# A two-layer diffusion block on one core: the start of the program rearranged (S5 loads, projection weights, modulation)

## The chip, the cores and the metric

The kernel runs on one core of one Trainium2 chip, as one program. The metric is the device time of one execution in microseconds (us). Before the change three runs took 2019.58, 2006.54 and 2016.45 us, median 2016.45. The engines are TensorE (PE), VectorE (DVE), ScalarE (ACT), GpSimd (POOL) and SyncE (SP). SP issues most transfers. ACT has a transfer queue of its own, and both queues issue in the order of their engine's instruction list.

## The reference

One latent stream of 512 tokens and a context of 256 tokens, 1024 wide, pass two layers. Layer 0 mixes with RWKV-7 heads and S5 channel groups that share one input projection `w_in`, layer 1 with latent attention; each layer ends in a mixture of experts. What matters here is the start of layer 0:

```
m_l = split(silu(c)     @ mod_w[0] + mod_b[0], 6)   # shift, scale, gate, ... for latent tokens
m_c = split(silu(c_ctx) @ mod_w[0] + mod_b[0], 6)   # the same for context tokens
a   = rmsnorm(h) * (1 + scale) + shift
p   = a @ w_in                                      # (768 x 1024) @ (1024 x 1792+512)
lam_bar = exp(lam * dt);  b_bar = ((lam_bar - 1) / lam) * b     # S5, per group of 16 channels
```

Everything is float32. `lam`, `dt`, `b` and `c` of S5 are small tables (2 directions, 32 groups, 64 states, 16 channels): 256 KB for each part of `b` and of `c`.

## The kernel before

The kernel is written in a tile framework that plans the order: the order in which the source calls operations sets priorities, and a planner with simulated times decides in which order the instructions then stand on each engine. Within one engine (and one queue) that order is fixed and is kept on the chip, whatever is ready.

`front` (L1795) runs the start. The 768 tokens are six tiles of 128 rows. For each tile: SP loads x (L1811, four buffers), ACT squares and sums it (L207), DVE and ACT make the reciprocal root (L217 to 221), ACT scales the rows (L1815), PE turns the tile in eight 128x128 transposes into two PSUM banks (L271, name nx), and ACT copies one half to `xT` (L276), DVE the other (L274).

Between tiles 2 and 3 `mod_part(0, 0)` (L139) stands: 16 loads of 512 KB of `mod_w` (name mw, L161, three buffers), each followed by four matmuls into one PSUM bank (psmod, L163); then DVE adds the bias and multiplies by the norm's weight (mo, L166 and L168), SP stores the result to DRAM (mods, L170), and `modcols` (L262) loads it back with channels on partitions (mcol).

`s5_tables` (L782) loads the S5 parameters through ACT's queue (L788 to L891), computes on DVE a long chain of small operations on 128x32 tiles (edt, emag, pw, co), then on 128x512 the product of `co` with `b` (s5tm, s5bb, L775 to L780), and turns the parts of c on PE (s5tc, L869). Before, `b` is loaded as 128 x 32 x 16, in pieces of 64 bytes.

`norm_mod` (L278) applies scale and shift to `xT` on POOL, 16 operations, and then splits each of eight channel blocks into a rounded high part (aT, ACT, L183) and a low part (DVE, L184). With aT the projection `w_in` starts: four blocks of weights (wi, L315, 512 KB each, two buffers), split in the same way (wih on ACT, wil on DVE), three matmuls per product into pwi (L189 to L191), and DVE's convolution into q (L327, L329).

After that come the S5 quads and 14 projection blocks, `mod_part(0, 1)` and `(0, 2)`, the RWKV stages (until about 940 us), `mod_part(1, 0..2)` inside the last of them (48 more loads of mw in the window 760 to 915 us), the output projection, the experts and layer 1.

Of the kernel before, what the change touches and what calls it, by code (L numbers as in the profile page):

```python
# [3 lines left out]


# [2 lines left out]

# [8 lines left out]
F32 = mybir.dt.float32  # L17
# [69 lines left out]
class Block:  # L87
# [50 lines left out]
    def mod_part(self, l, q, wpool, spool, tag="mod"):  # L138

        nc, i = self.nc, self.i  # L140
        if l not in self.mods:
            self.mods[l] = self.dr.tile([2, 6 * D], F32, name=f"mods{l}")
        dst = self.mods[l]
        mb = spool.tile([128, 512], F32, name=f"mb{l}{q}", tag="mb", bufs=1)
        nc.gpsimd.memset(mb, 0.0)
        for v in range(2):
            nc.sync.dma_start(mb[v::32, :], dap(i["mod_b"], l * 6 * D + q * 2048, [[512, 4], [1, 512]]))
        if q != 1:
            gm = spool.tile([128, 512], F32, name=f"gm{l}{q}", tag="gm", bufs=1)
            nc.gpsimd.memset(gm, 1.0)  # L150
            r0 = 64 if q == 0 else 0
            for v in range(2):
                nc.sync.dma_start(gm[r0 + v:r0 + 64:32, :], dap(i["norm1_g" if q == 0 else "norm2_g"], l * D,
                                                                [[512, 2], [1, 512]]))
            nc.vector.tensor_scalar(mb[r0:r0 + 64, :], mb[r0:r0 + 64, :], 1.0, None, op0=OP.add)
        ps = self.psum(tag, f"psmod{l}{q}", 1)
        for k in range(8):
            for h in range(2):
                wt = wpool.tile([128, 4, 256], F32, name=f"mw{l}{q}{k}{h}", tag="mw")
                w = i["mod_w"][l, k * 128:(k + 1) * 128, q * 2048:q * 2048 + 2048].rearrange("p (j c) -> p j c", j=4)  # L160
                nc.sync.dma_start(wt, w[:, :, 256 * h:256 * h + 256])  # L161
                for j in range(4):
                    nc.tensor.matmul(ps[32 * j:32 * j + 32, 256 * h:256 * h + 256], self.cst[:, k, :], wt[:, j],  # L163
                                     start=(k == 0 and h == 0), stop=(k == 7), skip_group_check=True)
        mo = spool.tile([128, 512], F32, name=f"mo{l}{q}", tag="mo", bufs=1)
        nc.vector.tensor_tensor(mo, ps, mb, OP.add)  # L166
        if q != 1:
            nc.vector.tensor_tensor(mo, mo, gm, OP.mult)  # L168
        for v in range(2):
            nc.sync.dma_start(dap(dst, v * 6 * D + q * 2048, [[512, 4], [1, 512]]), mo[v::32, :])  # L170

    def bcast(self, pool, l, v, c, name, tag, bufs):
        t = pool.tile([128, D], F32, name=name, tag=tag, bufs=bufs)
# [84 lines left out]
    def modcols(self, l, pool):  # L258

        t = pool.tile([128, 2, 2, 8], F32, name=f"mcol{l}")  # L260
        for v in range(2):
            self.nc.sync.dma_start(t[:, v], dap(self.mods[l], v * 6 * D, [[8, 128], [D, 2], [1, 8]]))  # L262
        return t

    def norm_x(self, xT, xn, t):

        nc = self.nc
        for h in range(2):
# [4 lines left out]
            if h:  # L273
                nc.vector.tensor_copy(dst, src)  # L274
            else:
                nc.scalar.activation(dst, src, AF.Copy)  # L276

    def norm_mod(self, aT, xT, mc):  # L278

        nc = self.nc  # L280
        for k in range(8):
            for v, c in ((1, slice(0, CTX)), (0, slice(CTX, T))):
                nc.gpsimd.tensor_scalar(xT[:, k, c], xT[:, k, c], mc[:, v, 1, k:k + 1], mc[:, v, 0, k:k + 1],
                                        op0=OP.mult, op1=OP.add)
            self.split(aT[0][:, k], aT[1][:, k], xT[:, k])

    def norm_tile(self, x, r, t, mc, pool):
# [18 lines left out]
                self.split(aT[0][:, ks], aT[1][:, ks], p3)  # L306
        return aT

    def w_in(self, aT, ms, wpool, hpool, qpool, done):

        nc, i = self.nc, self.i
        w = i["hy_w_in"]
        for m in ms:
            wt = wpool.tile([128, 8, 128], F32, name=f"wi{m}", tag="w")
            nc.sync.dma_start(wt, w[0, :, m * 128:(m + 1) * 128].rearrange("(p k) c -> p k c", k=8))  # L315
            wh = hpool.tile([128, 8, 128], F32R, name=f"wih{m}", tag="wh")
            wl = hpool.tile([128, 8, 128], F32R, name=f"wil{m}", tag="wl")
            self.split(wh, wl, wt)
# [463 lines left out]
    def s5_tables(self, cp, tp):  # L782
# [57 lines left out]
        self.a8 = self.c0.tile([128, 32], F32, name="s5a8")  # L840
        nc.vector.tensor_copy(self.a8, mag[:, 32:64])

        b = [tp.tile([128, 32, 16], F32, name=f"s5b{k}") for k in range(2)]
        for k, nme in enumerate(("s5_b_re", "s5_b_im")):
            nc.scalar.dma_start(b[k], dap(i[nme], 0, [[16, 128], [2048, 32], [1, 16]]))
        co = [tp.tile([128, 32], F32, name=f"s5co{k}") for k in range(2)]
        den = tp.tile([128, 32], F32, name="s5den")
        nc.vector.tensor_tensor(den, lr, lr, OP.mult)
# [946 lines left out]
    def front(self, qd, es):  # L1795
# [5 lines left out]
        with ExitStack() as e0:  # L1801
# [3 lines left out]
            with ExitStack() as e1:  # L1805
# [1 line left out]
                self.cond(xp)  # L1807
                xT = xp.tile([128, 8, T], F32, name="xT")
                for t in range(6):
                    xt = xp.tile([128, D], F32, name=f"x{t}", tag="x", bufs=4)  # L1810
                    nc.sync.dma_start(xt, self.src_rows(t))  # L1811
                    if t == 3:
                        self.mod_part(0, 0, mp, ms)
                    r = self.rstd_of(xp, xt, f"n0{t}")
                    nc.scalar.activation(xt, xt, AF.Copy, scale=r)  # L1815
                    self.norm_x(xT, xt, t)
                self.prep_cols(xp)
                self.s5_tables(c5, self.pool("s5p", 1, es=e1, side="right"))
                self.norm_mod(aT, xT, self.modcols(0, xp))
            wp = self.pool("wpb", 2, es=e0)  # L1820
            w5 = self.pool("s5w", 1, es=e0, side="right")
# [3 lines left out]
            rt = self.pool("s5rt", 1, es=e0, side="right")  # L1825
            self.s5_quad(0, w5)
            self.s5_quad(1, w5)
            self.w_in(aT, MS14[4 * 0:4 * 0 + 4], wp, hp, qp, take)
            self.s5_rot(rt)
            self.w_in(aT, MS14[4 * 1:4 * 1 + 4], wp, hp, qp, take)  # L1830
            self.mod_part(0, 1, mp, ms)
# [288 lines left out]
```

## Time and profile before

| what | value |
|---|---|
| runs | 2019.58, 2006.54, 2016.45 us (median 2016.45) |
| profiled execution | 2017.53 us, span 2015.5 us |
| TensorE's mean granted clock | 0.855 of full speed |
| busy share of the span | PE 79%, DVE 62%, POOL 39%, ACT 38% |
| transfers | 350.79 MB, mean 174 GB/s |
| `mod_w` loads | 96 of 512 KB, the largest group of transfers |

The shares are means over stages with different limits, so each stage is read by itself: in the first 100 us no engine is busy throughout, from 100 to 200 us DVE is, from 250 to 300 us PE is. A timeline row gives start, duration, engine (a q behind the name is that engine's transfer queue), line, operation, output and inputs, count, and in brackets the idle time before it and what ended it.

### The profile page before, as it was taken

The numbers are of one execution on the slowest core, as the hardware profiler recorded it, in microseconds if no ns is written. First come the engines' busy times: TensorE is split into PE (matmuls) and PEld (weight loads), VectorE is DVE, ScalarE is ACT, GpSimd is POOL, SyncE is SP. The second block draws the span as 40 slices with busy tenths as digits, with TensorE's granted clock in tenths as the row PEclk, the third lists the DMA queues.
The fourth block names the chain that finished last, engine by engine and source line by source line (L and its number), as shares of the span: only waits on it lengthen the run. The fifth ranks groups of instructions, "written<-read, shape, count | busy, mean of one in ns | idle before, by whom it ended". The sixth has DMA issues, their size and how long they took to land. (4 is left out here: it accounts for less than half of the span.)

```text
span 2015.5 us, 32393 instructions
## 1 busy us (share of the span) xinstructions
PE 1588.1 (79%) x12499; PEld 1151.5 (57%) x12499; DVE 1247.4 (62%) x2353; ACT 768.4 (38%) x1374; POOL 778.5 (39%) x732
## 2 busy tenths in 40 slices
PE   3688898477865857764979899967789998788993
PEld 2376767366755744433856666636655555666662
DVE  3799733986669485426365555657677874565554
ACT  4222323343443432213131554632456543325552
POOL 0577802572546351110333323534124444414432
PEclk9688899558967976876979999987879998889997
DMA  8654677723323316776631799963000006539974
GB/s 228 191 175 139 212 244 212 216 71 91 93 66 86 91 48 195 236 243 205 229 142 60 284 382 347 369 227 134 1 0 1 0 1 259 201 115 356 375 261 178
DMA packets 232581, 350.79 MB, mean 174 GB/s; under 512 B 57794, under 2 KB 178552, under 8 KB 217576
## 3 DMA queue, kind: packets, MB, share of 16 engines
q1 hardware_dynamic: 208944, 297.89, 44.3%
q0 software_dynamic: 10080, 44.04, 6.1%
q10 hardware_dynamic: 13400, 6.75, 1.2%
q8 instruction: 100, 1.64, 0.3%
q14 instruction: 57, 0.47, 0.1%
HBM read 280.60 MB, written 68.03 MB: 173 GB/s over the span
## 5 line engine op out<-in xcount | busy, mean ns | idle before, releaser
L163 PE MATMUL psmod<-mw,cst 128*32 128x256 f32 x768 | 81.6, 499 | 46.8 <-DMA mw<-in_mod_w_dram 46.7
L189 PE MATMUL pwi<-aT,wih 128*128 128x512 f32 (+1 forms) x224 | 83.4, 374 | 12.0 <-DVE q L329 12.0
L571 POOL TENSOR_TENSOR G<-G,gmask 128x1024 f32<-128x1024 f32 x24 | 58.9, 2458 | 80.7 <-ACT G L570 80.5
L191 PE MATMUL pwi<-aT,wil 128*128 128x256 f32 (+1 forms) x224 | 81.8, 366 | 0.0
L190 PE MATMUL pwi<-aT,wih 128*128 128x256 f32 (+1 forms) x224 | 81.6, 365 | 0.0
L1079 PE MATMUL s5y<-s5tq,s5H 128*96 128x128 f32 x256 | 52.4, 351 | 31.4 <-POOL s5H L1071 17.8
L1751 ACT ACTIVATE P<-st 128x512 f32<-128x512 f32 x96 | 56.9, 596 | 49.5 <-PE st L1749 46.1
L1382 POOL DMA_INDIRECT xg<-fbuf,rk x36 | 37.6, 1043 | 96.4 <-PE ptx L229 57.3
L1764 POOL TENSOR_TENSOR sum<-sum,P 128x512 f32<-128x512 f32 x48 | 63.6, 1348 | 28.2 <-ACT P L1751 28.0
L163 PEld LDWEIGHTS psmod<-mw,cst 128*32 128x32 f32 x768 | 19.9, 124 | 89.7 <-DMA mw<-in_mod_w_dram 65.9
L183 ACT ACTIVATE xT<-ptx 128x512 fp32r<-128x512 f32 x72 | 41.2, 596 | 68.1 <-PE ptx L229 67.7
L567 PE MATMUL pg<-PQ,KB 64*128 64x128 f32 x384 | 51.2, 352 | 14.9 <-ACT ta L496 10.1
L1079 PEld LDWEIGHTS s5y<-s5tq,s5H 128*96 128x96 f32 x256 | 41.4, 216 | 37.5 <-POOL s5H L1071 20.5
L184 DVE TENSOR_TENSOR xT<-ptx,xT 128x512 fp32r<-128x512 f32 x72 | 48.1, 687 | 22.1 <-ACT xT L183 21.2
L1762 POOL TENSOR_TENSOR sum<-P,P 128x512 f32<-128x512 f32 x16 | 20.5, 1301 | 106.5 <-ACT P L1751 106.4
L189 PEld LDWEIGHTS pwi<-aT,wih 128*128 128x128 f32 x224 | 47.1, 212 | 22.8 <-issue 13.7
L728 POOL TENSOR_TENSOR vo<-vo,bsum 128x512 f32<-128x512 f32 x6 | 6.2, 1042 | 134.3 <-DMA vo<-vtok 125.9
L229 PEld LDWEIGHTS ptx<-ident,xg 128*128 128x128 f32 x288 | 41.1, 193 | 28.0 <-issue 22.1
L567 PEld LDWEIGHTS pg<-PQ,KB 64*128 64x128 f32 x384 | 43.9, 244 | 22.2 <-ACT ta L496 10.4
L1755 PE MATMUL po<-P,vv 128*64 128x512 f32 x192 | 54.3, 617 | 1.1 <-ACT P L1751 1.1
L229 PE MATMUL ptx<-ident,xg 128*128 128x128 f32 x288 | 43.4, 286 | 12.4 <-issue 8.3
L190 PEld LDWEIGHTS pwi<-aT,wih 128*128 128x128 f32 x224 | 46.9, 209 | 6.8 <-issue 1.6
(1564 smaller groups left out, 5254.0 us busy)
## 6 DMA issues: line engine op xcount, KB each, us to landing
mw<-in_mod_w_dram SPq DMA_DIRECT2D x96, 512.0 KB
yb<-yo SPq DMA_DIRECT2D x36, 512.0 KB
s5tq<-s5t SPq DMA_DIRECT2D x16, 960.0 KB
yb<-zrow SPq DMA_DIRECT2D x16, 512.0 KB
wi<-in_hy_w_in_dram SPq DMA_DIRECT2D x14, 512.0 KB
rk<-qbuf SPq DMA_DIRECT2D x12, 512.0 KB
fbuf<-f SPq DMA_DIRECT2D x10, 512.0 KB
s5t<-s5CP SPq DMA_DIRECT2D x4, 1152.0 KB
```

The source lines that it names most:

```text
L163: nc.tensor.matmul(ps[32 * j:32 * j + 32, 256 * h:256 * h + 256], self.cst[:, k, :], wt[:, j], start=(k == 0 and h == 0), stop=(k == 7), s ...
L184: nc.vector.tensor_tensor(lo, src, hi.bitcast(F32), OP.subtract)
L189: nc.tensor.matmul(out, lh, rh, start=start, stop=False, **kw)
L190: nc.tensor.matmul(out, lh, rl, start=False, stop=False, **kw)
L191: nc.tensor.matmul(out, ll, rh, start=False, stop=stop, **kw)
L229: nc.tensor.transpose(pt[:, k * 128:(k + 1) * 128], a[:, h * 4 + k::8], self.ident)
L567: nc.tensor.matmul(pg[hp][:, m], KB[rs, m, ps2], PQ[rs, m, ps2], start=True, stop=True, skip_group_check=True)
L571: nc.gpsimd.tensor_tensor(G[:, par], G[:, par], self.mask[:, z, par, None, :].to_broadcast([128, 8, 128]), OP.mult)
L1079: nc.tensor.matmul(out, H[:, g, d, k, h0:h0 + 96], CP[:, k, d, i0:i0 + 8, :].rearrange("p a b -> p (a b)"), start=False, stop=(d == 1 and ...
L1751: ex = nc.scalar.activation(P, st, AF.Exp, scale=SCALE)
L1755: mm = nc.tensor.matmul(po[64 * x:64 * x + 64], vv[:, kt, h0 + x, :], P, start=(kt == 0), stop=(kt == 5), skip_group_check=True)
L1764: nc.gpsimd.tensor_tensor(sums[x], sums[x], P, OP.add)
```

## The change

- The transfers of `s5_tables` are all placed behind the last ACT copy of the input norm (`issue_after(normed)`), on ACT's queue as before.
- `b` is loaded as 32 rows of 8 KB and turned by 2 x 16 transposes on PE into two PSUM banks of tag "tp", from which DVE then reads it.
- The first four projection weights are issued behind the last load of `mod_part(0, 0)`.
- The six x tiles have six buffers in place of four.
- The store of mods and the load of mcol of this first part go through ACT's queue in place of SP's.
- `norm_mod` works on DVE for even channel blocks and on POOL for odd ones.

```diff
@@ mod_part
-                nc.sync.dma_start(wt, w[:, :, 256 * h:256 * h + 256])
+                last = nc.sync.dma_start(wt, w[:, :, 256 * h:256 * h + 256])
...
-            nc.sync.dma_start(dap(dst, v * 6 * D + q * 2048, [[512, 4], [1, 512]]), mo[v::32, :])
+            (nc.sync if l + q else nc.scalar).dma_start(dap(dst, v * 6 * D + q * 2048, [[512, 4], [1, 512]]), mo[v::32, :])
+        return last.ins
@@ modcols
-            self.nc.sync.dma_start(t[:, v], dap(self.mods[l], v * 6 * D, [[8, 128], [D, 2], [1, 8]]))
+            (self.nc.sync if l else self.nc.scalar).dma_start(t[:, v], dap(self.mods[l], v * 6 * D, [[8, 128], [D, 2], [1, 8]]))
@@ norm_mod
         for k in range(8):
+            eng = nc.gpsimd if k % 2 else nc.vector
             for v, c in ((1, slice(0, CTX)), (0, slice(CTX, T))):
-                nc.gpsimd.tensor_scalar(xT[:, k, c], xT[:, k, c], mc[:, v, 1, k:k + 1], mc[:, v, 0, k:k + 1],
-                                        op0=OP.mult, op1=OP.add)
+                eng.tensor_scalar(xT[:, k, c], xT[:, k, c], mc[:, v, 1, k:k + 1], mc[:, v, 0, k:k + 1],
+                                  op0=OP.mult, op1=OP.add)
@@ w_in
-            nc.sync.dma_start(wt, w[0, :, m * 128:(m + 1) * 128].rearrange("(p k) c -> p k c", k=8))
+            with self.tc.issue_after(behind) if behind is not None else nullcontext():
+                nc.sync.dma_start(wt, w[0, :, m * 128:(m + 1) * 128].rearrange("(p k) c -> p k c", k=8))
@@ s5_tables
-        b = [tp.tile([128, 32, 16], F32, name=f"s5b{k}") for k in range(2)]
+        b = []
         for k, nme in enumerate(("s5_b_re", "s5_b_im")):
-            nc.scalar.dma_start(b[k], dap(i[nme], 0, [[16, 128], [2048, 32], [1, 16]]))
+            raw = tp.tile([32, 2048], F32, name=f"s5br{k}")
+            nc.scalar.dma_start(raw, dap(i[nme], 0, [[2048, 32], [1, 2048]]))
+            pt = self.psum("tp", f"s5tb{k}", 2)
+            for c in range(16):
+                nc.tensor.transpose(pt[:, c * 32:c * 32 + 32], raw[:, c::16], self.ident[:32, :32])
+            b.append(pt.rearrange("p (c n) -> p n c", n=32))
@@ front
-                    xt = xp.tile([128, D], F32, name=f"x{t}", tag="x", bufs=4)
+                    xt = xp.tile([128, D], F32, name=f"x{t}", tag="x", bufs=6)
...
-                        self.mod_part(0, 0, mp, ms)
+                        loads = self.mod_part(0, 0, mp, ms)
...
-                    self.norm_x(xT, xt, t)
+                    normed = self.norm_x(xT, xt, t)
...
-                self.s5_tables(c5, self.pool("s5p", 1, es=e1, side="right"))
+                with self.tc.issue_after(normed):
+                    self.s5_tables(c5, self.pool("s5p", 1, es=e1, side="right"))
...
-            self.w_in(aT, MS14[4 * 0:4 * 0 + 4], wp, hp, qp, take)
+            self.w_in(aT, MS14[4 * 0:4 * 0 + 4], wp, hp, qp, take, loads)
```

The planner rearranges much behind these few lines: the lists of all engines differ from the start to about 940 us, and are alike from there on. Three places carry the prediction.

First ACT in the norm. Before (s5b and s5cr are transfers of b and c, x ... n00r the scaling of a tile, xT the copy of a turned tile):

```order
L207 ACTIVATE n02q,n02s<-x_161 128x1024
L845 DMA s5b_508<-in_s_b_re_dram 128x32x16
L845 DMA s5b_509<-in_s_b_im_dram 128x32x16
L868 DMA s5cr_541<-in_s_c_re_dram 128x1x64
L276 ACTIVATE xT<-nx_123 128x4x128
L1815 ACTIVATE x_135<-x_135,n01r 128x1024
```

Now, the end of the norm on ACT and what follows:

```order
L277 ACTIVATE xT<-nx_339 128x4x128
L1824 ACTIVATE x_351<-x_351,n05r 128x1024
L277 ACTIVATE xT<-nx_365 128x4x128
L792 DMA s5rows<-in_s_lam_re_dram 32x128
L793 DMA s5rows<-in_s_lam_im_dram 32x128
L795 DMA s5ld<-in_s_log_dt_dram 32x2
L850 DMA s5br_508<-in_s_b_re_dram 32x2048
L850 DMA s5br_527<-in_s_b_im_dram 32x2048
L877 DMA s5cr_575<-in_s_c_re_dram 128x1x64 x2
```

The transfers of S5 stood between the first and the second copy of the norm, and stand now behind the sixth. Further down on ACT come one split (wih), the store of mods, a second split, the load of mcol, the eight splits of aT, and then eight transfers of the imaginary part of c.

Second DVE around the modulation. Before:

```order
L775 TENSOR_TENSOR s5tm_486<-s5b_508,s5co_512 128x512
L776 TENSOR_TENSOR s5tm_487<-s5b_509,s5co_513 128x512
L166 TENSOR_TENSOR mo_296<-psmod_199,mb_190 128x512
L777 TENSOR_TENSOR s5bb_530<-s5tm_486,s5tm_487 128x512
L168 TENSOR_TENSOR mo_296<-mo_296,gm_194 128x512
L778 TENSOR_TENSOR s5tm_486<-s5b_508,s5co_513 128x512
L779 TENSOR_TENSOR s5tm_487<-s5b_509,s5co_512 128x512
L780 TENSOR_TENSOR s5bb_531<-s5tm_486,s5tm_487 128x512
```

Then came four small ones for the heads and the eight low parts of aT. Now:

```order
L779 TENSOR_TENSOR s5tm_486<-s5tb_510,s5co_546 128x512
L780 TENSOR_TENSOR s5tm_487<-s5tb_529,s5co_547 128x512
L286 TENSOR_SCALAR xT<-xT,mcol_633 128x512 x4
L781 TENSOR_TENSOR s5bb_564<-s5tm_486,s5tm_487 128x512
L286 TENSOR_SCALAR xT<-xT,mcol_633 128x256 x4
L782 TENSOR_TENSOR s5tm_486<-s5tb_510,s5co_547 128x512
L783 TENSOR_TENSOR s5tm_487<-s5tb_529,s5co_546 128x512
L185 TENSOR_TENSOR aT_83<-xT,aT_82 128x768 x3
L784 TENSOR_TENSOR s5bb_565<-s5tm_486,s5tm_487 128x512
L185 TENSOR_TENSOR aT_83<-xT,aT_82 128x768 x5
L889 COPY s5dg<-s5td 128x8
```

DVE's half of the modulation stands inside the work on b. The two operations of mo, and two splits wil of projection weights, now stand earlier, inside the chain of small operations; behind aT stand s5dg and the small ones for the heads, the first product with c (s5q) and the first convolution (q).

Third SP at the end of the RWKV stages. Before:

```order
L161 DMA mw_9142<-in_mod_w_dram 128x4x256
L701 DMA yd_2712<-Y_8902 64x512
L701 DMA yd_2713<-Y_8902 64x512
L161 DMA mw_9148<-in_mod_w_dram 128x4x256
L161 DMA mw_9154<-in_mod_w_dram 128x4x256
L161 DMA mw_9160<-in_mod_w_dram 128x4x256
L734 DMA yo_9006<-yd_2713 128x512
L1902 DMA cz_9215<-s5buf 128x768
L161 DMA mw_9166<-in_mod_w_dram 128x4x256
```

Now:

```order
L161 DMA mw_9194<-in_mod_w_dram 128x4x256
L161 DMA mw_9200<-in_mod_w_dram 128x4x256
L705 DMA yd_2746<-Y_8837 64x512
L705 DMA yd_2747<-Y_8837 64x512
L170 DMA mods_7875<-mo_9206 4x512 x2
L705 DMA yd_2746<-Y_8936 64x512
L705 DMA yd_2747<-Y_8936 64x512
L738 DMA yo_9040<-yd_2747 128x512
```

yd and yo are the outputs of the last RWKV steps. The last 10 of the 48 loads of mw stood behind the store of the last step but one; now all 48 stand ahead of it. On PE the last eight groups of psmod stood behind all matmuls of RWKV and now stand ahead of the last step's.

## Rows read from the trace of the kernel before

**Rows 1.** timeline of ACT and its queue: start, us, operation, idle before

```profile
10.77 5.21 ACTq L845 DMA_DIRECT2D s5b<-in_s_b_im_dram  x1
...
16.02 8.44 ACTq L868 DMA_DIRECT2D s5cr<-in_s_c_re_dram  x1
24.51 0.60 ACT L276 ACTIVATE xT<-nx 128x512 f32<-128x512 f32 x1 [12.70 <-issue]
...
33.57 0.60 ACT L276 ACTIVATE xT<-nx 128x512 f32<-128x512 f32 x1 [0.22 <-PE nx L271]
...
42.59 0.60 ACT L276 ACTIVATE xT<-nx 128x512 f32<-128x512 f32 x1 [0.80 <-PE nx L271]
...
46.25 5.61 ACTq L868 DMA_DIRECT2D s5cr<-in_s_c_im_dram  x7
```

**Rows 2.** timeline of SP's queue

```profile
37.24 2.56 SPq L315 DMA_DIRECT2D wi<-in_hy_w_in_dram  x2
39.91 25.02 SPq L161 DMA_DIRECT2D mw<-in_mod_w_dram  x13
...
66.50 1.08 SPq L170 DMA_DIRECT2D mods<-mo  x2
...
69.97 0.89 SPq L262 DMA_DIRECT2D mcol<-mods  x2
```

**Rows 3.** timeline of PE

```profile
44.58 0.53 PE L795 MATMUL s5t<-ident,s5rows 32*128 32x32 f32 x3
...
46.19 1.08 PE L163 MATMUL psmod<-mw,cst 128*32 128x256 f32 x8
...
63.42 1.08 PE L163 MATMUL psmod<-mw,cst 128*32 128x256 f32 x8 [0.34 <-DMA mw<-in_mod_w_dram]
...
69.77 1.08 PE L163 MATMUL psmod<-mw,cst 128*32 128x256 f32 x8 [0.75 <-DMA mw<-in_mod_w_dram]
```

**Rows 4.** timeline of DVE

```profile
10.94 0.42 DVE L155 TENSOR_SCALAR mb<-mb 64x512 f32<-64x512 f32 x1 [1.11 <-DMA mb<-in_mod_b_dram]
...
40.46 0.89 DVE L894 TENSOR_TENSOR s5glu<-s5gw,s5m 128x128 f32<-128x128 f32 x4
...
45.14 0.26 DVE L797 COPY s5lam<-s5t 128x96 f32<-128x96 f32 x1 [0.23 <-PE s5t L795]
...
62.34 0.29 DVE L780 TENSOR_TENSOR s5pw<-s5tm,s5tm 128x128 f32<-128x128 f32 x1
...
64.56 0.69 DVE L166 TENSOR_TENSOR mo<-psmod,mb 128x512 f32<-128x512 f32 x1 [0.60 <-PE psmod L163]
...
80.66 8.99 DVE L184 TENSOR_TENSOR aT<-xT,aT 128x768 fp32r<-128x768 f32 x8 [11.54 <-ACT aT L183]
...
97.39 0.47 DVE L327 SCALAR_TENSOR_TENSOR q<-pwi,cols,q 128x255 f32<-128x255 f32 x1
```

**Rows 5.** groups of DVE by shape, 30 to 100 us: count, busy, mean ns, idle

```profile
L184 DVE TENSOR_TENSOR wil<-wi,wih 128x1024 fp32r<-128x1024 f32 x2 | 2.5, 1225 | 1.0 <-ACT wih L183 1.0
```

**Rows 6.** timeline of POOL

```profile
73.21 14.58 POOL L283 TENSOR_SCALAR xT<-xT,mcol 128x512 f32<-128x512 f32 x16 [6.17 <-DMA mcol<-mods]
```

**Rows 7.** groups of POOL by shape, 60 to 100 us

```profile
L283 POOL TENSOR_SCALAR xT<-xT,mcol 128x256 f32<-128x256 f32 x8 | 8.6, 1085 | 0.0
L283 POOL TENSOR_SCALAR xT<-xT,mcol 128x512 f32<-128x512 f32 x8 | 6.0, 764 | 6.2 <-DMA mcol<-mods 6.2
```

**Rows 8.** windows: length, busy of PE, PEld, DVE, ACT, POOL, clock, DMA share, GB/s

```profile
100.00:125.00 25.00, 20.75 (x128) 16.58 (x128) 25.00 (x44) 7.30 (x12) 20.84 (x18) 1.00 0.56 191
...
250.00:300.00 50.00, 50.00 (x320) 34.34 (x319) 15.03 (x27) 11.79 (x23) 4.81 (x8) 1.00 0.77 231
...
850.00:900.00 50.00, 37.12 (x652) 21.56 (x652) 19.61 (x42) 10.22 (x20) 5.07 (x5) 0.76 0.76 237
```

**Rows 9.** timeline of SP's queue at the end of RWKV

```profile
901.62 5.28 SPq L161 DMA_DIRECT2D mw<-in_mod_w_dram  x3
```

**Rows 10.** waits of PE, 760 to 940 us: total us, times, longest

```profile
PE psmod L163 <- DMA mw<-in_mod_w_dram: 30.7, 20, 5.0
```

More of the change, by code (lines that the diff above doesn't have):

```diff
@@ L6 @@
 import math
-from contextlib import ExitStack
+from contextlib import ExitStack, nullcontext
 import concourse.bacc as _bacc
@@ L275, in norm_x @@
             else:
-                nc.scalar.activation(dst, src, AF.Copy)
+                last = nc.scalar.activation(dst, src, AF.Copy)
+        return last.ins
     def norm_mod(self, aT, xT, mc):
@@ L307, in norm_tile, with w_in @@
         return aT
-    def w_in(self, aT, ms, wpool, hpool, qpool, done):
+    def w_in(self, aT, ms, wpool, hpool, qpool, done, behind=None):
         nc, i = self.nc, self.i
```

## The prediction

> **What bounds the kernel now.** I read the windows first, because the busy shares of the page mix stages. From 100 to 125 us DVE is busy all 25.00 us, and from 250 to 300 us PE is busy all 50.00 us [rows 8]. So whatever makes the first 100 us shorter is passed on: DVE starts its full stretch earlier, and PE its own after it. Then I read the timelines of the first 100 us, engine by engine, looking for the operation that lets DVE begin on aT, and going back from there.
>
> The low parts of aT start on DVE at 80.66 and end at 80.66 + 8.99 = 89.65, after an idle time of 11.54 us in which DVE waited for ACT's high parts [rows 4]. Those waited for POOL's modulation, which started at 73.21 after a wait for mcol [rows 6]. Mcol waited for the store of mods, issued at 66.50, and this for the last group of psmod, which ended at 63.42 + 1.08 = 64.50 [rows 2, 3]. From the store's issue to POOL's start it is 73.21 - 66.50 = 6.7 us. The groups of psmod follow the loads: from 46.19 to 69.77 thirteen groups begin, (69.77 - 46.19)/12 = 1.97 us for each 512 KB [rows 3]. The stream began late for two reasons. ACT stood 12.70 us before its first copy of the norm, behind two issues of S5 transfers of 5.21 and 8.44 us on its queue [rows 1]. And two pairs of projection weights stand in SP's order between the loads of mw, the second at 37.24 [rows 2].
>
> The S5 chain on DVE runs from 45.14 to 62.34 + 0.29 = 62.63 [rows 4]. It ends 1.9 us before psmod, so it is a second path of nearly the same length.
>
> **The norm and the loads of mw.** The first copy on ACT could have started at 24.51 - 12.70 = 11.81. Copies follow each other at (33.57 - 24.51)/3 = 3.02 us [rows 1], so the sixth would start at 11.81 + 5 x 3.02 = 26.9 and end at 27.5, in place of 42.59 + 0.60 = 43.19. Six x buffers let the fifth and sixth tile be issued in time.
>
> The first psmod can follow the first tile's transposes at about 13, one group of 1.08 behind 11.81. Then 16 loads of mw and the last two x tiles share the queue: 18 x 1.97 = 35.4, so the last psmod ends at 48.4. The 32 transposes of b are new on PE. Three of the same kind took 0.53 [rows 3], so 16 take 2.8 us. A group of psmod takes 1.08 of 1.97 us, which leaves 0.89 that hides part; three buffers hide more. Left uncovered, they cost 2 x (2.8 - 0.9) = 3.8. I take 0.6, and 49 for psmod's end (44.4 if the x tiles cost nothing, 54 with both losses and a later start). That is 15.5 earlier.
>
> **Mods and mcol.** The two operations of mo take 1.4 (two at 0.69 [rows 4]). On ACT a split of projection weights now stands ahead of the store. Its weights are issued behind the last mw, and the split takes about what wil takes, 1.2 [rows 5]. So mcol is there at 49 + 1.4 + 1.2 + 6.7 = 58.3 (53 to 64). The change of queue itself I cost at nothing: SP's store went out at 66.50, 1.9 after mo's first operation began at 64.56, which mo's own two operations and the one between them nearly fill [rows 2, 4].
>
> **The S5 chain.** Its loads are now issued at 27.5, three small ones first. Issue and landing I bound by the 6.7 us of the store and load in series, and from below by half of that, 3.35. Before, the chain began 1.95 after the norm's end. So it starts at 27.5 + 1.95 + 5 = 34.5 (33 to 39). It takes 62.63 - 45.14 = 17.5. Into it now come 0.89 of s5glu [rows 4], 1.4 of mo and two wil at 1.225, together 4.7 [rows 4, 5]. Then s5tm twice, 1.4. DVE reaches the modulation at 34.5 + 17.5 + 4.7 + 1.4 = 58.1 (56 to 63). The two paths meet at 58.3, against 73.21 before: **14.9 earlier** (10 to 17).
>
> **Modulation and aT.** Before, 73.21 to 89.65, 16.4 us. DVE's new list is 8 modulations, 4 operations on b of 0.69 and 8 low parts of aT. No row shows the modulation on DVE; the nearest is a tensor_scalar of 64x512 at 0.42 [rows 4]. From below it is 8 x 0.42 + 4 x 0.69 + 8.99 = 15.1. From above POOL's half comes on top, if the two engines take turns: 4 x 0.764 and, for the 256 wide, 4 x 0.4 by halving, 4.7 in all [rows 7], so 19.8. That two engines slow each other is in the rows. POOL's operation on 512 columns took 764 ns while DVE was idle (the eight of them end before 80.66), and the one on 256 columns took 1085 ns beside DVE's low parts [rows 7]. I take 16.4, nearer the lower end, since the 8.99 already has POOL beside it. The end of aT comes at 74.7, still 14.9 earlier.
>
> The Trainium skill, "SBUF — State Buffer", section "Who interferes with whom", says that a VectorE tensor_scalar in its two-port mode, or one with two SBUF inputs, and a GpSimd operation that reads SBUF exclude each other for the whole instruction. The 1085 against 764 ns agree with it. By that rule POOL's 4.7 us are bought with DVE's time, the stage is 19.8 and aT ends at 78.1.
>
> **Behind aT.** Small S5 operations that before filled DVE's wait for mcol now stand behind aT: nine of at most 0.26 and one of at most 0.69 by the nearest rows [rows 4], I take 1.5. A larger cost is the first convolution. It came at 97.39, 7.7 us after aT [rows 4], because the projection needs that long; DVE filled the time with S5 products. Now only one product (of c's real part) stands ahead of it, and the next needs the imaginary part, whose eight transfers are issued on ACT behind the splits of aT: 8 x 5.61/7 = 6.4 us [rows 1]. Also c can be turned only when DVE has read b out of the two PSUM banks. So DVE waits up to 7.7 - 2.0 = 5.7 us, or nothing if the projection begins early on finished blocks; I take 2.9.
>
> Sum of the front: 14.9 - 1.5 - 2.9 = **10.5 us gained**. Ends: 17 + 1.3 - 1.5 = 16.8, and 10 - 3.4 - 1.5 - 5.7 = -0.6.
>
> **The end of RWKV.** Between 760 and 915 us 48 loads of mw run beside the RWKV steps. The DMA share is 0.76 from 850 to 900 [rows 8], PE waited 30.7 us in 20 waits for them, 5.0 at most [rows 10]. Ten of these loads leave the place behind the last step but one and go ahead of it, on SP as on PE. The step's output no longer waits behind the three loads that took 5.28 [rows 9]: a gain of up to 5.3. But the last step on PE now waits for the eight groups that stood behind everything: 8 x 1.97 = 15.7 at most, nothing where the share of 0.76 leaves room. The stage starts 10 us earlier too. I take zero between -5.3 and +15.7. Everything behind 940 us stands in the same order, and I cost it at nothing.
>
> **Forecast.** The profiled execution took 2017.53, 1.1 above the median. 2017.5 - 10.5 = **2007.0** against it; I say 2006 against the median.
>
> **Rivals.**
> - *The last RWKV step waits for mw.* For it: the longest wait of 5.0 in a stage where loads and not PE set psmod's pace; all 48 now stand ahead of the step. Against: a quarter of the DMA time was free. Price 15.7, so 2006 + 15.7 = 2022, slower than before. It decides from 10.5 us on, that is when more than five of the eight groups are waited for in full. Chance 0.18.
> - *DVE takes the gain back* at the start: the S5 chain in DVE's order starts late, the two engines take turns in the modulation, and q waits in full. For it: both paths are of nearly the same length, and 1085 against 764 ns. Front gain near the lower end, about 2: 2014. If turns alone come true (the skill's page above), 10.5 - 3.4 = 7.1 remain, 2009. Chance 0.17.
> - *The pieces of the change do not land as ordered:* the mw stream stays late, for instance because transposes of b and S5's small packets hold it. Then mods are issued at 60 or later, and the time is that of before, 2016. Against: no row puts anything else ahead of the stream. Chance 0.07.
> - *A larger gain:* 16.8 at the front and 5.3 at the tail, 22 in all, 1994. For it: DVE's and PE's full stretches pass all of it on. Chance 0.20.
> - The forecast, 2006 (2000 to 2012): 0.38.
>
> What a measurement of this kernel can tell from no change is about 1%, 20 us; the runs of before differ by 13. Under 1996.3 lie most of the fourth rival and a little of the forecast: 0.20. Over 2036.6 only more than the first rival's full price, and a rearranged middle that I have not priced: 0.08. The range takes in the first rival with a margin and most of the larger gain: 1989 to 2023.
>
> **What would show it.** ACT's first copy near 12 without an idle time behind issues; the sixth at 27. Psmod of the first part ended by 49, mcol landed by 58, aT's last low part near 75, and a wait of DVE for pwi of about 3 us behind it. The modulation on DVE at 0.4 us each says that the engines share; 0.8 or more, that they take turns. PE full from about 240 on. At the tail PE's total wait for mw, 30.7 before, tells the first rival. I am wrong if aT ends before 70 or after 84, or if the stretch from 100 to 940 us changes its length by more than 10.

## The result, and the profile after

The changed kernel takes 1990.72 us (median of 4 runs, 1987.68 to 1993.2) against 2014.57 for the kernel before: ratio 0.989, interval [0.9866, 0.9915]. The time lies inside the stated range, near its lower end. The gain is 24 us where 10.5 were forecast. In the profiled executions the spans are 1989.7 and 2015.5, 25.8 apart, and the positions below are from these.

The first part went nearly as forecast. ACT and its queue, in the timeline of the changed kernel:

```profile
13.50 0.57 ACT L277 ACTIVATE xT<-nx 128x512 f32<-128x512 f32 x1
...
26.68 0.60 ACT L277 ACTIVATE xT<-nx 128x512 f32<-128x512 f32 x1 [0.80 <-PE nx L272]
...
31.53 9.80 ACTq L877 DMA_DIRECT2D s5cr<-in_s_c_re_dram  x8
...
52.49 1.31 ACTq L170 DMA_DIRECT2D mods<-mo  x2
...
58.26 1.32 ACTq L263 DMA_DIRECT2D mcol<-mods  x2
```

The first copy of the norm stands at 13.50, without the idle time of 12.70 behind the issues, and the sixth at 26.68 [rows 1]. SP's queue:

```profile
14.43 30.27 SPq L161 DMA_DIRECT2D mw<-in_mod_w_dram  x13
44.75 1.67 SPq L319 DMA_DIRECT2D wi<-in_hy_w_in_dram  x2
```

Thirteen loads of mw now follow each other without projection weights between them, 30.27/13 = 2.33 us each. PE and DVE:

```profile
36.44 1.08 PE L163 MATMUL psmod<-mw,cst 128*32 128x256 f32 x8 [3.46 <-DMA mw<-in_mod_w_dram]
...
37.58 1.92 PE L853 MATMUL s5tb<-ident,s5br 32*128 32x32 f32 x16
...
49.88 1.08 PE L163 MATMUL psmod<-mw,cst 128*32 128x256 f32 x8 [1.29 <-DMA mw<-in_mod_w_dram]
```

```profile
37.80 0.26 DVE L801 COPY s5lam<-s5t 128x96 f32<-128x96 f32 x1 [4.23 <-PE s5t L799]
...
51.03 0.69 DVE L166 TENSOR_TENSOR mo<-psmod,mb 128x512 f32<-128x512 f32 x1 [1.92 <-PE psmod L163]
...
62.01 2.67 DVE L286 TENSOR_SCALAR xT<-xT,mcol 128x512 f32<-128x512 f32 x4 [0.71 <-DMA mcol<-mods]
...
65.19 2.69 DVE L286 TENSOR_SCALAR xT<-xT,mcol 128x256 f32<-128x256 f32 x4
...
72.20 4.42 DVE L185 TENSOR_TENSOR aT<-xT,aT 128x768 fp32r<-128x768 f32 x5
...
84.34 0.46 DVE L331 SCALAR_TENSOR_TENSOR q<-pwi,cols,q 128x255 f32<-128x255 f32 x1
```

The last psmod of the first part ends at 49.88 + 1.08 = 50.96, in place of 64.50. The S5 chain starts at 37.80, since the transposes of s5rows stand on PE behind a group of psmod that waited 3.46 us for its load. DVE reaches the modulation 0.71 us before mcol lands: the two paths meet at 62.0, nearly together, as they were to (58.3 in the forecast). aT ends at 72.20 + 4.42 = 76.62, 13.0 us earlier, and the first q comes at 84.34, 13.05 earlier. ACT's half of the first q, on which DVE's half waits, before and now:

```profile
93.82 0.47 ACT L326 ACTIVATE q<-pwi,cols 128x256 f32<-128x256 f32 x1 [5.16 <-PE pwi L191]
```

```profile
83.22 0.47 ACT L330 ACTIVATE q<-pwi,cols 128x256 f32<-128x256 f32 x1 [9.56 <-PE pwi L192]
```

Modulation by shape on both engines (count, busy, mean ns):

```profile
L286 DVE TENSOR_SCALAR xT<-xT,mcol 128x512 f32<-128x512 f32 x4 | 2.7, 728 | 0.7 <-DMA mcol<-mods 0.7
...
L286 DVE TENSOR_SCALAR xT<-xT,mcol 128x256 f32<-128x256 f32 x4 | 2.7, 732 | 0.0
...
L286 POOL TENSOR_SCALAR xT<-xT,mcol 128x512 f32<-128x512 f32 x4 | 4.4, 1118 | 9.1 <-DMA mcol<-mods 9.1
```

and POOL's stretch of it in the timeline:

```profile
62.17 6.67 POOL L286 TENSOR_SCALAR xT<-xT,mcol 128x512 f32<-128x512 f32 x8 [9.13 <-DMA mcol<-mods]
```

POOL is done at 62.17 + 6.67 = 68.84, having waited 9.13 for mcol.

The full stretches are still full, of DVE from 100 and of PE from 250:

```profile
100.00:125.00 25.00, 24.83 (x154) 20.16 (x152) 24.83 (x53) 6.58 (x11) 14.97 (x13) 0.93 0.65 218
250.00:300.00 50.00, 49.68 (x350) 34.68 (x342) 14.94 (x23) 11.74 (x20) 0.00 (x0) 1.00 1.00 301
850.00:900.00 50.00, 25.67 (x470) 17.37 (x465) 14.79 (x25) 10.61 (x19) 0.98 (x1) 0.67 0.51 152
```

The share of DMA time from 850 to 900, 0.76 before, is 0.51, since the 48 loads now end earlier, at 867. Four milestones on PE, first in the kernel before and then in the changed one (after the count: shortest, median and longest ns, then first and last start in us):

```profile
L191 PE MATMUL pwi<-aT,wil x224: 274/392/628, 85.0 to 302.8; 128*128 128x256 f32 x58, 128*128 128x512 f32 x54
...
L491 PE MATMUL plo<-q,wu x192: 272/272/580, 334.5 to 714.5; 64*128 64x128 f32 x192
...
L567 PE MATMUL pg<-PQ,KB x384: 272/373/580, 372.4 to 767.5; 64*128 64x128 f32 x192
...
L1910 PE MATMUL ptcat<-ident,cy x24: 272/421/449, 928.9 to 951.5; 128*128 128x128 f32 x24
```

```profile
L192 PE MATMUL pwi<-aT,wil x224: 274/392/632, 73.1 to 285.8; 128*128 128x256 f32 x56, 128*128 128x512 f32 x56
...
L495 PE MATMUL plo<-q,wu x192: 272/272/579, 310.6 to 694.9; 64*128 64x128 f32 x192
...
L571 PE MATMUL pg<-PQ,KB x384: 272/417/579, 346.7 to 776.4; 64*128 64x128 f32 x192
...
L1920 PE MATMUL ptcat<-ident,cy x24: 272/421/447, 904.1 to 927.9; 128*128 128x128 f32 x24
```

The last pwi comes 17.0 us earlier, the first plo 23.9, the first pg 25.7, the first ptcat 24.8. So 13 us are there at the start, and nearly 13 more are won by the first pg. PE's waits from 85 to 400 us show part of where, before and after:

```profile
PE plo L491 <- DMA q<-q2d: 14.9, 1, 14.9
...
PE pg L567 <- ACT ta L496: 10.1, 1, 10.1
```

```profile
PE plo L495 <- DMA q<-q2d: 7.2, 1, 7.2
PE pg L571 <- ACT ta L500: 5.1, 1, 5.1
```

plo waits half as long for its q, and pg half as long for ta. The last step of RWKV in SP's timeline:

```profile
880.66 1.12 SPq L705 DMA_DIRECT2D yd<-Y  x2
883.61 0.34 SPq L738 DMA_DIRECT2D yo<-yd  x1
```

PE's waits from 760 to 940 (total, count, longest, in us):

```profile
PE psmod L163 <- DMA mw<-in_mod_w_dram: 27.5, 22, 5.3
```

From the step's yd to its yo it is 2.95 us; before, the three loads of 5.28 stood between them [rows 9]. PE's wait for mw is 27.5, against 30.7 [rows 10].

### The profile page after: what moved, and what is told of

Same layout as the page of the kernel before. It is cut to its first block, busy times and chain, and to the rows that moved or that the text cites. A ratio compares the mean times of both kernels' runs of the same rounds, so it can differ in the third digit from the quotient of the medians.

```text
span 1989.7 us, 32476 instructions
## 1 busy us (share of the span) xinstructions
PE 1595.7 (80%) x12531; PEld 1154.8 (58%) x12531; DVE 1241.2 (62%) x2361; ACT 767.6 (39%) x1375; POOL 767.2 (39%) x724
## 5 line engine op out<-in xcount | busy, mean ns | idle before, releaser
L190 PE MATMUL pwi<-aT,wih 128*128 128x256 f32 (+1 forms) x224 | 82.7, 371 | 10.2 <-DVE q L333 9.3
L1088 PE MATMUL s5y<-s5tq,s5H 128*96 128x128 f32 x256 | 59.3, 373 | 34.3 <-POOL s5H L1078 17.3
L191 PE MATMUL pwi<-aT,wih 128*128 128x256 f32 (+1 forms) x224 | 81.8, 367 | 0.0
L163 PEld LDWEIGHTS psmod<-mw,cst 128*32 128x32 f32 x768 | 19.9, 123 | 91.1 <-DMA mw<-in_mod_w_dram 65.6
L192 PEld LDWEIGHTS pwi<-aT,wil 128*128 128x128 f32 x224 | 47.0, 210 | 6.9 <-issue 2.1
```

The lines of the kernel that those rows point to most:

```text
L190: nc.tensor.matmul(out, lh, rh, start=start, stop=False, **kw)
L191: nc.tensor.matmul(out, lh, rl, start=False, stop=False, **kw)
L192: nc.tensor.matmul(out, ll, rh, start=False, stop=stop, **kw)
L1088: nc.tensor.matmul(out, H[:, g, d, k, h0:h0 + 96], CP[:, k, d, i0:i0 + 8, :].rearrange("p a b -> p (a b)"), start=False, stop=(d == 1 and ...
```

## The experiments

Times are medians. A ratio is to runs of the kernel before that were taken beside it; their medians differ (2008 to 2015), so ratios are compared. Positions are in us and from one execution of each kernel. Those of e2, e5 and e9 took 7 to 8 us more than the median of their kernel, so their positions and spans may stand late by up to that.

| kernel | aT ends | first q | last pwi | first plo | first pg | last pY | first ptcat | span | ratio [interval] |
|---|---|---|---|---|---|---|---|---|---|
| before | 89.65 | 97.39 | 302.8 | 334.5 | 372.4 | 899.1 | 928.9 | 2015.5 | 1 |
| changed | 76.62 | 84.34 | 285.8 | 310.6 | 346.7 | 879.7 | 904.1 | 1989.7 | 0.989 [0.9866, 0.9915] |
| e1_plo_early | 88.40 | 96.13 | 302.5 | 331.9 | 367.9 | 879.2 | 910.0 | 1995.7 | 0.9942 [0.9916, 0.9969] |
| e2_plo_late | 75.25 | 83.07 | 287.1 | 316.4 | 355.1 | 893.5 | 917.6 | 2007.4 | 0.9941 [0.9921, 0.9961] |
| e3_behind_alone | 87.44 | 95.17 | 297.4 | 329.1 | 367.0 | 908.3 | 932.4 | 2015.8 | 1.0037 [1.002, 1.0054] |
| e4_not_behind | 79.23 | 82.92 | 294.2 | 315.6 | 350.1 | 868.5 | 892.7 | 1981.0 | 0.9867 [0.9837, 0.9897] |
| e5_new_front_old_rest | 71.45 | 103.25 | 305.3 | 337.0 | 374.8 | 905.8 | 936.3 | 2021.4 | 1.0006 [0.9986, 1.0025] |
| e6_old_front_new_rest | 90.27 | 96.60 | 304.1 | 329.0 | 365.1 | 893.6 | 917.9 | 2001.1 | 0.9938 [0.9914, 0.9962] |
| e7_neutral | 76.20 | 86.30 | 287.4 | 317.3 | 359.3 | 894.9 | 919.2 | 2000.0 | 0.9964 [0.9943, 0.9985] |
| e8_dve_alone | 78.50 | 86.18 | 283.6 | 310.9 | 351.4 | 869.8 | 899.4 | 1989.8 | 0.9893 [0.9854, 0.9931] |
| e9_slow_after | 90.87 | 97.75 | 300.2 | 325.1 | 361.3 | 895.8 | 919.8 | 2002.5 | 0.9928 [0.9898, 0.9958] |
| e10_slow_before | 102.85 | 110.57 | 315.5 | 347.2 | 385.1 | 909.5 | 939.6 | 2023.5 | 1.0066 [1.0038, 1.0094] |
| e11_rows_alone | 86.71 | 95.83 | 294.8 | 318.1 | 353.0 | 883.7 | 914.7 | 1999.8 | 0.9967 [0.9945, 0.9988] |
| e12_no_rows | 81.56 | 88.63 | 288.0 | 317.9 | 358.7 | 868.8 | 892.9 | 1979.2 | 0.9843 [0.9805, 0.9882] |

My theory after the result was: the 13 us of the first part are passed on, and the rest comes from the other order in which the planner put the later instructions, mainly from plo, which stands behind 116 of the 192 matmuls of the S5 projection and stood behind 158. The rival: the earlier front itself removes waits further on.

**plo's place.** In the kernel before, plo put earlier; in the changed one, later:

```diff
-                    self.mm3(ps[:, :n], ...)                       # pws, block m from 2.5 on
+                with self.tc.issue_after(self.plo0) if m + a / 768 > 2.2 else nullcontext():
+                    ...
```

> The kernel before, with one order forced on PE: the last two and a half halves of the S5 projection (pws) stand behind the first eight matmuls of plo, which so stand behind 120 of the 192 pws matmuls and not behind 158. Theory 1 (the part of the gain that the front does not explain comes from where plo stands): plo begins 38 x 0.175 = 6.7 us earlier, near 328, the first pg follows near 366, and the time falls by 5 to 8 us to about 2008. Theory 2 (it comes from waits that the earlier front itself removes, on DVE, SP and the loads): plo waits for its q and wu, and the time stays within 3 us of before, 2014.

```diff
-        self.st[0] = self.rwkv_stage_a(0, self.sp, self.wa, ("ca", "bs"), 1)
-        self.w_in_s5(aT, wp, hs, up)
+        late = self.w_in_s5(aT, wp, hs, up, range(3))
+        with self.tc.issue_after(late):
+            self.st[0] = self.rwkv_stage_a(0, self.sp, self.wa, ("ca", "bs"), 1)
+        self.w_in_s5(aT, wp, hs, up, range(3, 4))
```

> The changed kernel, with plo put behind three of four blocks of the S5 projection, 144 of 192 matmuls in place of 116. Theory 1: plo begins 28 x 0.175 = 4.9 us later, near 315.5, and the time rises by 4 to 6 us to about 1995.5. Theory 2: plo's later start is taken up by other waits behind it and the time stays within 2 us of 1990.7.

plo came 2.6 us earlier in e1 (6.7 expected) and 5.8 later in e2 (4.9 expected). The first pg followed by -4.5 and +8.4. But the time moved by far more: e1's last pY comes 19.9 us earlier, e2's 13.8 later. One forced place made the planner arrange all of RWKV anew, and that moved as much as plo did, or more. So the place of plo counts, but neither run isolates it.

**Which part frees the front.** One part alone, or all but one:

```diff
@@ e3_behind_alone, on the kernel before
+                with self.tc.issue_after(normed):
+                    self.s5_tables(c5, self.pool("s5p", 1, es=e1, side="right"))
@@ e4_not_behind, on the changed kernel
-                with self.tc.issue_after(normed):
+                self.s5_tables(c5, self.pool("s5p", 1, es=e1, side="right"))
@@ e11_rows_alone, on the kernel before: the s5_tables part of the change
@@ e12_no_rows, on the changed kernel: that part undone
```

> The kernel before with one part of the change alone: all S5 transfers behind the last copy of the input norm, b still in pieces of 64 bytes. Theory 1 (the stall of ACT behind the issues was the head of the chain): the first copy comes near 12 us, the sixth near 30, the last psmod of the first part ends by 56, aT by 81 to 84, and the time is 2005 to 2009. Rival (the pieces of b are the cost wherever they stand): ACT's issues take 13 us behind the norm, s5lam or the products with b come late, aT ends at 87 or later and the time stays at 2012 or above.

> The changed kernel without the placing of S5's transfers behind the norm; b still comes in rows of 8 KB. Theory 1: ACT stands behind its transfer issues again, the first copy comes at 20 or later, aT ends near 84, the time is about 1998 to 2003. Rival (the rows alone had removed the stall, since 13.65 us of issue time stood at b and right behind it): the first copy comes before 15, aT ends within 3 us of 76.6, the time stays near 1991.

In e3 ACT no longer stands behind the issues, but the pieces of b and c do not cost less there. ACT and its queue in e3's timeline:

```profile
14.09 0.57 ACT L276 ACTIVATE xT<-nx 128x512 f32<-128x512 f32 x1
...
33.26 4.68 ACTq L846 DMA_DIRECT2D s5b<-in_s_b_im_dram  x1
37.98 11.06 ACTq L869 DMA_DIRECT2D s5cr<-in_s_c_re_dram  x8
```

and SP's queue there:

```profile
24.29 39.74 SPq L161 DMA_DIRECT2D mw<-in_mod_w_dram  x13
```

Thirteen loads of mw took 39.74 us, 3.06 each, against 25.02 for thirteen before [rows 2] and 30.27 in the changed kernel. The projection weights still stand among the first ones. So the last psmod ends only 0.9 us earlier, at 63.60, and aT 2.2 earlier. The rival was right, with aT at 87.44. In e4 the rival was right too: the first copy came at 12.12 though the transfers stand among ACT's norm again, and aT ends 2.6 later than in the changed kernel.

> The kernel before with b in rows of 8 KB and turned on PE, nothing else. After the two runs on the placing behind the norm, theory 1a: the rows are what removes ACT's stall. The first copy comes before 15, the last psmod of the first part before 58, aT ends by 82. Rival: ACT still stands behind the transfers of c, the first copy at 18 or later, aT ends at 86 or later. The time as a whole may land anywhere from 1990 to 2015 by the order of the later lists.

> The changed kernel with b in pieces of 64 bytes again, all else as changed (S5's transfers behind the norm, projection weights behind the loads of mw). Theory 1a: the pieces run beside the loads of mw and take their time on the transfer engines, the last psmod of the first part ends at 55 or later in place of 51, aT ends at 82 or later. Rival (the placing of the projection weights is what freed the stream): aT ends within 3 us of 76.6.

In e11 the rows alone remove the stall, 5.21 us of issue become 0.67:

```profile
10.26 0.67 ACTq L846 DMA_DIRECT2D s5br<-in_s_b_im_dram  x1
...
11.82 0.60 ACT L276 ACTIVATE xT<-nx 128x512 f32<-128x512 f32 x1
...
39.79 0.60 ACT L276 ACTIVATE xT<-nx 128x512 f32<-128x512 f32 x1 [0.80 <-PE nx L271]
...
69.82 8.87 ACTq L873 DMA_DIRECT2D s5cr<-in_s_c_im_dram  x7
78.79 5.98 ACT L183 ACTIVATE aT<-xT 128x768 fp32r<-128x768 f32 x8 [8.40 <-DMA mw<-in_mod_w_dram]
```

With four x buffers and the projection weights in the stream the sixth copy comes at 39.79. The last psmod still ends at 57.94, 6.6 us earlier than before, and POOL's modulation starts at 64.48, 8.7 earlier. But aT ends at 86.71, past the 82 expected: in this order the issues of c's imaginary part stand on ACT ahead of the splits of aT, which begin 14.3 us behind the modulation's start, against 6.6 before (79.79 - 73.21). So the 2.9 us at aT are not what the rows are worth; a new place of other transfers took most of their gain back. In e12, all but the rows, the last psmod ends at 54.19 and aT at 81.56, each just short of what theory 1a asked and well past the rival's 79.6.

At aT's end, then, the placing behind the norm alone gives 2.2, the rows alone 2.9, all parts together 13.0; without the rows 8.1 are left, without the placing 10.4. e11 and e4 both have the rows and not the placing. Between their 2.9 and 10.4 lie the other four parts: projection weights behind mw, six x buffers, the queue of mods and the split modulation. Of these only the split was undone by itself (below); what each of the others is worth stays open.

**Front and lists apart.** A table in the kernel holds what is traced behind aT, on each engine and queue, in the order of the other kernel (`traced` is the list of instructions as the source makes them, `_LATER` the wanted order):

```diff
+    for packed in _LATER.values():
+        ...
+            if last is not None:
+                tc.add_manual_dep(traced[at], last.name, ...)   # issue order only
+            last = traced[at]
```

> The changed kernel's first part (all that is traced up to aT), with everything traced behind it held, engine by engine and queue by queue, in the order in which it stands in the kernel before. Theory 1 (the earlier front is passed on in full, and what is more comes from the order of the later lists): aT ends near 76, the first q comes near 84, the last pwi near 289, the time falls by 11 to 15 us against before, ratio 0.9925 to 0.9945. Theory 2 (the gain is in the later order, the earlier front only ends in other waits): the ratio is 0.998 or more. Theory 3 (the earlier front is worth all of it, the lists nothing): 0.9885 or less.

> The kernel before, its first part as it was, with everything traced behind aT held in the order of the changed kernel. Theory 1: aT ends near 89, and the later order alone gives the 9 to 13 us that the front does not explain, ratio 0.9935 to 0.9955. Theory 2: 0.990 or less. Theory 3: 0.998 or more.

e6 gives the lists without the front: 0.9938, and by its row in the table plo comes 5.5 us earlier, pg 7.3, pY 5.5, ptcat 11.0. e5 seems to say that the front is worth nothing. Its DVE timeline shows why it does not measure that:

```profile
68.77 2.68 DVE L188 TENSOR_TENSOR aT<-xT,aT 128x768 fp32r<-128x768 f32 x3
...
90.22 0.17 DVE L892 COPY s5dg<-s5td 128x8 f32<-128x8 f32 x1 [13.09 <-PE s5td L890]
```

aT ends at 71.45, 18 us earlier than before, but in the old list the small operations on s5dg stand ahead of all work on q. They wait 13.09 us for a transpose of s5td, which stands on PE behind the first projection matmuls. So DVE idles just where it is to be full, and the first q comes 5.9 later than before. The two halves don't fit; the run is told for that and for one thing more. Its store of mods and load of mcol stand on ACT's queue as in the changed kernel, but hardly a transfer runs beside them, and the modulation begins at 57.83, 5.2 behind the store in place of 9.5. ACT's queue in e5, then the window from 52 to 56 us, first of the changed kernel and then of e5 (the last two numbers are the share of the transfer engines' time and GB/s):

```profile
52.65 1.13 ACTq L173 DMA_DIRECT2D mods<-mo  x2
...
54.47 1.02 ACTq L266 DMA_DIRECT2D mcol<-mods  x2
```

```profile
52.00:56.00 4.00, 0.95 (x8) 0.23 (x8) 3.79 (x21) 1.76 (x2) 0.83 (x2) 0.50 1.11 342
```

```profile
52.00:56.00 4.00, 0.00 (x0) 0.00 (x0) 3.78 (x18) 1.94 (x2) 0.99 (x2) 0.50 0.13 33
```

The question is put anew by slowing the front, with every list held as it is:

```diff
+                mc = self.modcols(0, xp)
+                ...                                            # slow: a tile of 128x512, sl: a tile like mc
+                for n in range(16):
+                    nc.vector.tensor_copy(slow[:, 32 * n:32 * n + 32], mc.rearrange("p a b c -> p (a b c)"))
+                for n in range(24):
+                    nc.vector.tensor_scalar(slow, slow, 1.0, None, op0=OP.mult)
+                nc.vector.tensor_copy(sl, slow[:, 0:32].rearrange("p (a b c) -> p a b c", a=2, b=2))
-                self.norm_mod(aT, xT, self.modcols(0, xp))
+                self.norm_mod(aT, xT, sl)
```

> The changed kernel with all its lists held as they are and 41 operations put into DVE's list ahead of the modulation, which needs their result: the first part ends later by their time, about 13 us, and nothing else moves. If the time of the first part is passed on in full, aT ends near 90, the last pwi and plo come 13 us later too, and the time rises by 11 to 14 us over 1990.7, to 2002 to 2005. If the lists hold the rest to other waits, it rises by less than 5 us.

> The kernel before with its lists held and the same 41 operations ahead of aT on DVE, and ahead of the modulation on POOL: the first part ends about 13 us later. Passed on in full: the time rises to about 1.006 to 1.007 of before. Held by other waits: below 1.0025.

DVE's timeline of the changed kernel, slowed:

```profile
86.45 4.42 DVE L188 TENSOR_TENSOR aT<-xT,aT 128x768 fp32r<-128x768 f32 x5
```

and its ptcat on PE:

```profile
L1933 PE MATMUL ptcat<-ident,cy x24: 272/421/447, 919.8 to 942.3; 128*128 128x128 f32 x24
```

aT ends 14.25 later, plo 14.5, pg 14.6, ptcat 15.7, the span 12.8 longer; by the ratios 0.9928 against 0.989, about 8 us, with intervals that just overlap. This 8 lies between the two outcomes named beforehand, 11 to 14 and less than 5. The kernel before, slowed by 13.2 at aT: 12.7 at plo, 10.7 at ptcat, 8.0 in the span, 1.0066 by the ratio, 13 us, which is the outcome called passed on in full. So most of the time in the first part is passed on; whether all of it is, these runs can't tell.

**How much an order is worth by itself.**

```diff
                 self.cond(xp)
+                nc.vector.memset(xp.tile([128, 512], F32, name="spare"), 0.0)
```

> The changed kernel with one memset of 128x512 on DVE at the start, about 0.3 us beside the first loads, which nothing reads. The planner's lists differ from about the 126th place on PE on, in the projection and the RWKV stages. Theory 1 (the order that the planner happens to find is worth up to 10 us either way): aT ends within 1 us of 76.6, and the time still moves by 4 to 15 us against 1990.7, up or down. Theory 3: it stays within 3 us.

aT ends 0.4 us from where it did, and the time rises from 0.989 to 0.9964, 15 us. plo comes 6.7 later, pg 12.6, ptcat 15.1. PE's list is the same up to its 367th instruction, at 86 us; what differs is the order behind it.

**The modulation.**

```diff
-            eng = nc.gpsimd if k % 2 else nc.vector
+            eng = nc.vector
```

> The changed kernel with all 16 operations of the modulation on DVE and none on POOL. If the two engines took turns, an operation on DVE alone is much shorter than the 0.67 us that it took beside POOL, 0.25 to 0.45, the 16 take 4 to 7 us, and the stage from the first modulation to the end of aT stays at 14 to 16 us though half the hands are gone. If they worked side by side, it takes 0.67 again, 16 take 10.7, and the stage grows to about 20 us. The time as a whole moves with the planner's later order and is not predicted better than 1985 to 2000.

The same groups of DVE with POOL idle:

```profile
L286 DVE TENSOR_SCALAR xT<-xT,mcol 128x512 f32<-128x512 f32 x8 | 3.7, 540 | 2.3 <-DMA mcol<-mods 2.3
L286 DVE TENSOR_SCALAR xT<-xT,mcol 128x256 f32<-128x256 f32 x8 | 2.7, 402 | 0.0
```

and, in the changed kernel, aT's products, which start at 69.00, behind POOL's last operation:

```profile
L185 DVE TENSOR_TENSOR aT<-xT,aT 128x768 fp32r<-128x768 f32 x8 | 7.1, 946 | 0.0
```

Alone DVE takes 540 and 402 ns; beside POOL it took 728 and 732, and POOL's 512 columns went from 764 [rows 7] to 1118. From the first modulation to aT's end it is 78.50 - 62.83 = 15.7 us, against 14.6 with both engines and 16.4 with POOL alone before. The whole time did not move: 0.9893. The second pair of hands is worth 1.1 us: the first outcome named beforehand, with the stage at 14 to 16 us on one engine as on two.

## Why the prediction was right, and where it was off

- **The chain of the first part** held in its order of events, with psmod, the modulation and aT 2 to 4 us late. Sixth copy: 26.9 forecast, 26.68 measured. Last psmod's end: 49, measured 50.96. Modulation: 58.3, measured 62.0. aT's end: 74.7, measured 76.62. The loads ran at 2.33 us each and not 1.97. ACT's S5 transfers ran beside them and the transposes of b stood on PE between the groups of psmod; no run separates the two, and in e4, where S5's transfers are issued by 26 us, it is still 29.43/13 = 2.26. The transposes of b took 1.92 and 1.97 on PE, below the 2.8 assumed.
- **Mods to mcol** was mis-sized: 6.7 forecast, and 62.0 - 52.49 = 9.5 measured. ACT's load of mcol was issued at 58.26, 5.8 behind the store of mods and not 3.5 as before [rows 2], because SP's list no longer waits between the two and keeps the transfer engines busy with wi and the next mw. I had costed the change of queue at nothing. e5 above shows that the load beside it is the cost and not the queue. In the changed kernel it cost little, because the S5 chain came no earlier: 61.3 in place of 58.1, with s5lam at 37.80 and not 34.5.
- **Modulation and aT** took 14.6, 0.5 below my lower end of 15.1. That the engines slow each other was right: DVE's operations beside POOL took 0.73 us, between the 0.4 that was to mean sharing and the 0.8 that was to mean turns. 16 operations took DVE 6.4 us alone (3.7 + 2.7 by the rows of e8), and the 8 and 8 took from 62.01 to 68.84 with one product of b between them. By the Trainium skill, "SBUF — State Buffer", section "Who interferes with whom", a VectorE operation in its two-port mode and a GpSimd operation exclude each other for the whole instruction. The runs agree with that in direction and not in full measure: by their times alone, 4 x (0.54 + 0.40) on DVE and 4 x (0.76 + 0.55) on POOL (the kernel before, where three operations of 256 columns ran at 550 ns as DVE's low parts were only beginning), turns would have taken 9.0 us, and both were done in 6.8. Nor did a stage of 19.8 come: my sum had counted POOL's time on top of low parts of 1.12 us each, which already stood beside POOL, and alone they take 0.95 (the row of 946 ns above).
- **Behind aT** I took off 4.4 us. None of it was lost at the first q: it comes 7.7 us behind aT in both kernels. That the two are equal is luck, and my reading that the projection needs that long was wrong for the kernel before. ACT's half of that q, on which DVE's half waits, was done there at 93.82 + 0.47 = 94.29, 4.6 behind aT, and DVE's S5 products, which stand ahead of q in its order, held q until 97.39. Now it is done at 83.69, 7.1 behind aT, and q follows at 84.34. So DVE's waits there, 1.60 for s5td and 2.7 ahead of the heads, cost at most 0.65.
- **What failed is the step that costed the lists.** The forecast took the middle as unchanged and the tail as zero, and said that it would be wrong if the stretch from 100 to 940 us changed by more than 10. It did: 11.8 more by the first ptcat (24.8 - 13.0). By places: 4 us to the last pwi, 7 to plo, 2 to pg, then 6 lost by the last pY, 5.4 won from there to ptcat. The last is the term I bounded at 5.3 and took as zero, now out of the way of yo. All runs bear it out: from the last pY to the first ptcat it is 29.6 to 31.0 us in the six in which loads of mw stand on SP behind the last yd (before, e1, e5, e8, e10, e11), and 24.0 to 24.4 in the eight others (the last groups of psmod on PE follow these loads, so the two are not told apart). e6 shows that the order of what stands behind aT gives 12 us without any change in front; by its positions, about half of that is this term. e9 and e10 show by their ratios that of 14 and 13 us of delay in front 8 and 13 are passed on. So 8 to 13 of the gain come from the front and 12 from the order, 20 to 25 together, against 24 by the medians and 25.8 by the profiles. The two do not simply add: e5, the new front with the old order, gained nothing.
- **The rivals.** The last RWKV step did not wait for mw: PE's total is 27.5 in place of 30.7, and 1.9 of it falls in the 20 us up to that step's yd (860 to 882). DVE did not take the gain back. The larger gain came true in size (1994 worked out, 1990.7 measured), but not as I made it up: its front was to give 16.8 and gave 13.
- **What stays open.** Why the planner's order for the changed kernel is the better one is not settled beyond its places. e7 shows that it is not owed to what the change does: a memset that nothing reads takes 15 of the 24 us away again. e4 and e12, which undo a part of the change, have their aT end later and are as fast or faster as a whole (0.9867 and 0.9843, intervals that overlap the changed kernel's), as RWKV came out shorter, e12's from pg to ptcat by 23 us (534.2 against 557.4). TensorE's mean granted clock is higher in them too, 0.860 to 0.866 in their runs against 0.853 to 0.858 in the changed kernel's, and no run tells the clock's share from the order's. Of e12 alone the table says that it is the fastest version run, at 1978.95 us, and that its front is not why.

## What to carry to other kernels

Where a planner orders the lists, an edit has two effects: its own, which can be worked out from the trace, and a new order everywhere behind it, which took 15 us away here in e7 and gave 12 in e6, and which the rows of the trace before show only in part (here the loads ahead of yo). Put that second effect into the range as a term of its own, by timing one or two neutral edits, and judge an edit by its own stage (here the end of aT) or with the later order held. A single part of a change, run alone, can look worth little because something else takes its gain back: with the rows alone the modulation began 8.7 us earlier and aT ended only 2.9 earlier, since other issues then stood ahead of the splits. So read what the stage waits for in that run before calling the part small. And a small store and load in series is best kept clear of large loads: 9.5 us from store to modulation beside them, 5.2 without (e5).

## What the runs showed of the hardware

Large loads take longer beside small pieces: thirteen loads of 512 KB in a row took 25.02 us beside few of S5's transfers [rows 2], 30.27 beside S5's transfers with b in rows, 34.04 with b in pieces (e12), and 39.74 in e3. The second issue of b in 64-byte pieces held ACT's queue 5.21 us, in rows 0.67 (e11). A store to DRAM and the load behind it were issued 5.8 us apart with the transfer engines at a share of 1.11 and 1.8 apart at 0.13 (e5). Two engines on one SBUF tile cost each other: DVE's 256 columns took 402 ns alone and 732 beside POOL.
